# Attention scores of a hybrid decoder trunk: two PSUM banks per unit reduced, exponentiated and summed as one

## The chip, the cores and the metric

The kernel runs on one core of one Trainium2 chip. The metric is the time of one execution on the device in microseconds (us); lower is better. Five engines work from queues of their own, each in order: TensorE (PE, with its weight loads shown apart as PEld), VectorE (DVE), ScalarE (ACT), GpSimd (POOL) and SyncE (SP, which issues DMAs). Matmul results go to PSUM, which the kernel hands out as eight banks of 512 float32 columns by 128 partitions.

## The reference

Two layers over a sequence of 1024 tokens and a width of 1024. Each layer projects the normalised input once, runs three mixers side by side (a gated MLP over chunks, a state space mixer over chunks, and latent attention), joins them with an output projection, and adds a squared-ReLU MLP. All of it is float32. The change is in attention: six heads, query and key width 96, value width 64, blocks of 128 queries:

```python
def one_block(args):
    q_blk, blk = args
    s = jnp.einsum('bhqd,bkhd->bhqk', q_blk, k).astype(jnp.float32) * scale
    q_pos = blk * CHUNK + jnp.arange(CHUNK)
    s = jnp.where(k_pos[None, :] <= q_pos[:, None], s, -jnp.inf)
    p = jax.nn.softmax(s, axis=-1).astype(v.dtype)
    return jnp.einsum('bhqk,bkhd->bqhd', p, v)

out = lax.map(one_block, (qb, jnp.arange(nq)))
```

## The kernel before

Every float32 product is made of three matmuls on operands that are split into a high and a low part (`split`: ScalarE rounds the high part, VectorE subtracts). Most of the time goes to the output projection and the MLP (L1014); attention lies between the projections of a layer and its MLP.

Attention works on units (h,qt): head h of 6, query tile qt of 8, with w = 128 (qt + 1) keys each. A unit with qt of 0 to 3 is narrow and fits one PSUM bank of 512 columns. A unit with qt of 4 to 7 is wide and takes two banks, each with half of its keys. `scores` does a unit: three matmuls per bank, named `sc`, and one more that adds the causal mask to the last 128 keys; a VectorE maximum per bank (L767); for a wide unit a VectorE minimum of the two negated maxima (`mx`); a ScalarE exponential per bank that also sums its row (L780, with a reading of the accumulator of its own). `normalize` adds the two sums (`sm`), takes the reciprocal and multiplies the row, on POOL for all but qt 0. Then `p_t` transposes pieces of up to 512 columns of the result on TensorE (`pTp`) and splits them (`pT`), and `p_v` multiplies them by the values (`av`); a finished half of a head is copied out by ScalarE (`mixC`).

Units are issued in a fixed sequence: (0,0) to (0,3), and then for each head h (h,4), (h,5), (h+1,0), (h,6), (h,7), (h+1,1), (h+1,2), (h+1,3). Beside the first four, `q_tile` projects the last four of eight query tiles (`qps`, evacuated by ScalarE) and `prep_q0` transposes the first head's queries (`qT0`, which the profile shows as `qT`); later heads' queries are transposed eight tiles at a time (`qTp`), and near the end of attention `mix_a` transposes results of the other mixers (`mT`). Normalisation follows four units behind the scores (LAG), and p_v three pieces behind p_t (VKEEP).

The eight PSUM banks are handed out by tag: four to `a`, two to `b`, two to `c`. A bank is written again only when the readers of its last use are done. In attention the tag `a` serves `sc`, `qps`, `qTp` and `mT`; `b` serves `pTp` and `qT0`; `c` serves `av`. Outside of attention all eight banks serve the projections and the MLP.

The order in which each engine's instructions stand is not the order of the source: a scheduler plays the recorded program through with its own costs, takes what is ready first, and fixes one order for each engine. On the chip every engine follows that order and waits by semaphores.

Of the kernel before, what the change touches and what calls it, by code (L numbers as in the profile page):

```python
# [9 lines left out]
F32 = mybir.dt.float32  # L10
# [52 lines left out]
AHEAD = 2  # L63
MIX_FROM = 36


@with_exitstack
def trunk(ctx, tc, x, w_zdk, w_uv, w_f, w_q, w_kv, w_out, w1, w2, gains, pcol, prow, w_s, cst, out):
# [6 lines left out]
    gp = ctx.enter_context(tc.tile_pool(name="gp", bufs=N_G))  # L75
    ps = ctx.enter_context(tc.tile_pool(name="ps", bufs=2, space=PSUM))
    dram = ctx.enter_context(tc.tile_pool(name="dram", bufs=1, space=DRAM))

# [8 lines left out]
    def bank(tag, name):  # L87
        return ps.tile([P, 512], F32, tag=tag, name=name, bufs=BANKS[tag])

# [537 lines left out]
    def qkv(L):  # L627
# [27 lines left out]
        attention_setup(L)  # L655
        L.wq = weights(2, 0)

    def v_tile(L, t, o):
# [15 lines left out]
    def q_tile(L, t):  # L674
        cT, qv = L.cT, L.att[0]
        for n in range(2):
            o = bank("a", "qps")
            for k in range(3):
                whi, wlo = (q_[:, k * 288:(k + 1) * 288] for q_ in L.wq[n])
                a, b = (q_[:, t * P:(t + 1) * P] for q_ in cT[k])  # L680
                on = o[:, 0:288]
                mm(on, a, whi, k == 0, False)
                mm(on, a, wlo, False, False)
                mm(on, b, whi, False, k == 2)
            act.activation(qv[:, t, n * 288:(n + 1) * 288], o[:, 0:288], AF.Copy, scale=L.cr_q[:, t:t + 1])
# [40 lines left out]
    def prep_q(L, h):  # L726
# [3 lines left out]
        for half in range(2):  # L730
            pt = bank("a", "qTp")
            for t in range(4):
                tk = half * 4 + t
                pe.transpose(pt[0:r, t * P:(t + 1) * P], qv[:, tk, (h + 1) * QK - r:(h + 1) * QK], ident)
            sl = slice(half * 512, half * 512 + 512)
            split(qT[i][0][0:r, sl], qT[i][1][0:r, sl], pt[0:r])
# [7 lines left out]
    def attention(L, l, xsrc):  # L744
        vt = L.vt

        def scores(h, qt):
# [7 lines left out]
            wh = w // nh  # L755
            os = [bank("a", "sc") for _ in range(nh)]
            q0 = slice(qt * P, (qt + 1) * P)
            mx = small.tile([P, 2], F32, tag="mx", name="mx", bufs=8)
            for n in range(nh):
                on = os[n][:, :wh]  # L760
                ks = slice(n * wh, (n + 1) * wh)
                mm(on, qh[:, q0], kh[:, ks], True, False)
                mm(on, qh[:, q0], kl[:, ks], False, False)
                mm(on, ql[:, q0], kh[:, ks], False, n < nh - 1)
                if n == nh - 1:
                    mm(on[:, wh - P:], ident_r, maskq_r, False, True)
                dve.reduce_max(mx[:, n:n + 1], on, axis=AX.X, negate=True)  # L767
            if nh == 2:
                tt(mx[:, 0:1], mx[:, 0:1], mx[:, 1:2], ALU.min)
            sm = small.tile([P, 2], F32, tag="sm", name="sm", bufs=8)  # L770
            p0 = 0
# [6 lines left out]
            pw = p[:, p0:p0 + w]  # L778
            for n in range(nh):
                act.activation(pw[:, n * wh:(n + 1) * wh], os[n][:, :wh], AF.Exp, bias=mx[:, 0:1],  # L780
                               accum_out=sm[:, n:n + 1])
            return pw, sm, nh

        narrow = [None]

        def normalize(u, pw, sm, nh):
            if nh == 2:
                tt(sm[:, 0:1], sm[:, 0:1], sm[:, 1:2], ALU.add)
            sm = sm[:, 0:1]
            dve.reciprocal(sm, sm)  # L790
# [94 lines left out]
        for _ in mixing:  # L885
            pass
        R = mlp(L, l, xsrc)
        R.prep(1)
# [8 lines left out]
    def mix_a(L):  # L897
# [3 lines left out]
        for k in range(5):  # L901
            mk = G(F32, "mixA")
            for half in range(2):
                pt = bank("a", "mT")
                for t in range(4):
# [348 lines left out]
    for l in range(DEPTH):  # L1254
# [46 lines left out]
        del L.vv, L.wsv, L.vg, L.sg, L.dtb, L.alog, L.dsk  # L1301
        L = attention(L, l, xsrc).go()


# [73 lines left out]
```

## Time and profile before

| What | us |
|---|---|
| Time, median of 2 runs (2200.74 to 2202.67) | 2201.7 |
| The profiled execution's own time | 2201.31 |
| Its span, first to last instruction | 2199.5 |
| TensorE (PE) busy | 2171.2 |
| Weight loads (PEld) busy | 1846.9 |
| VectorE (DVE) busy | 1661.8 |
| ScalarE (ACT) busy | 1138.0 |
| POOL busy | 477.2 |

The profile is of one execution, which took 1.8 us more than its span. Times on a timeline count from the start of the span. Matmuls are pipelined: a row lasts from the start of one matmul to its last result, and the next one starts before that, so that a busy TensorE is not one at its peak, and its rows hide short waits.

### The profile page before, as it was taken

Reading aid. Unit: us, or ns where it says so; the run is one execution under the profiler, and the core shown is the slowest. Engines: PE = TensorE matmul, PEld = TensorE weight load, DVE = VectorE, ACT = ScalarE, POOL = GpSimd, SP = SyncE. Lnnn points to the kernel's source line nnn. Section 1 sums busy time; section 2 is a strip of 40 time slices with the busy share of each in tenths; the row PEclk is TensorE's granted clock in tenths of the full one; section 3 lists DMA queues with packets and bytes.
Section 4 is the critical chain, followed back from the end, with each engine's and each line's share of the span. In section 5 each row is a group of like instructions: output and inputs, shape, how many; then the busy total and the mean of one; then the engine's idle time right before and its main releaser. Section 6 shows DMA issues by size and latency. Waiting matters only on the chain.

```text
span 2199.5 us, 28731 instructions
## 1 busy us (share of the span) xinstructions
PE 2171.2 (99%) x10844; PEld 1846.9 (84%) x10844; DVE 1661.8 (76%) x2484; ACT 1138.0 (52%) x1867; POOL 477.2 (22%) x451
## 2 busy tenths in 40 slices
PE   9999999999999999999999999999999999999997
PEld 8888989888888888888898889998888888888886
DVE  7788588888776876767847867878888767677576
ACT  6364477556445445355533625775464453553543
POOL 4152266221010001001301613761110010011002
PEclk9999999999999999999999999999999999999999
DMA  5211301445565546545412113023565565356532
GB/s 175 75 53 57 87 1 48 98 125 138 121 130 138 128 100 140 147 89 125 156 50 70 54 45 75 1 96 68 135 153 122 106 140 147 88 125 144 136 75 77
DMA packets 64922, 222.16 MB, mean 101 GB/s; under 512 B 7600, under 2 KB 7952, under 8 KB 64784
## 3 DMA queue, kind: packets, MB, share of 16 engines
q0 software_dynamic: 20736, 75.51, 20.2%
q1 hardware_dynamic: 44048, 144.83, 19.9%
q8 instruction: 85, 1.39, 0.3%
q14 instruction: 53, 0.43, 0.1%
HBM read 211.87 MB, written 8.44 MB: 100 GB/s over the span
## 4 chain that ended last, share of the span: by engine, by line
PE 93%; DVE 4%; issue 2%; ACT 1%; DMA 1%; POOL 0%; SPq 0%; POOLq 0%; ACTq 0%; DVEq 0%
PE st L1014 60%; PE cqkv L119 5%; PE xbc L119 5%; PE uvps L119 4%; PE av L119 4%; PE sc L119 3%; PE zps L119 2%; PE pTp L805 2%; PE qps L119 2%; PE yps L119 1%; PE vps L119 1%; PE knps L119 1%; DVE hB L103 1%; DMA x<-in_x 1%; DVE mx L767 1%
## 5 line engine op out<-in xcount | busy, mean ns | idle before, releaser
L1014 PE MATMUL st<-bhi,wlo 128*128 128x512 f32 x2016 | 785.1, 389 | 0.0
L1014 PE MATMUL st<-blo,whi 128*128 128x512 f32 x2016 | 785.0, 389 | 0.0
L1014 PE MATMUL st<-bhi,whi 128*128 128x512 f32 x2016 | 778.1, 390 | 2.4 <-ACT bhi L115 2.4
L1014 PEld LDWEIGHTS st<-bhi,whi 128*128 128x128 f32 x2016 | 378.7, 188 | 81.1 <-ACT bhi L115 2.7
L1014 PEld LDWEIGHTS st<-blo,whi 128*128 128x128 f32 x2016 | 378.9, 188 | 78.7 <-DVE blo L100 0.5
L1014 PEld LDWEIGHTS st<-bhi,wlo 128*128 128x128 f32 x2016 | 378.7, 188 | 78.5
L206 POOL DMA_DIRECT2D ssum<-in_w x96 | 84.1, 876 | 937.5 <-DVE wlo L100 387.5
L100 DVE TENSOR_TENSOR wlo<-raw,whi 128x1024 fp32r<-128x1024 f32 (+4 forms) x189 | 237.2, 1256 | 54.2 <-issue 29.8
L100 DVE TENSOR_TENSOR x<-x,st 128x512 f32<-128x512 f32 x296 | 196.7, 683 | 30.2 <-PE st L1014 29.8
L115 ACT CAST bhi<-tsum 128x1024 fp32r<-128x1024 f32 x96 | 101.0, 1052 | 213.9 <-DVE tsum L100 172.9
L115 ACT CAST whi<-raw 128x1024 fp32r<-128x1024 f32 (+4 forms) x189 | 193.9, 1029 | 16.0 <-DVE blo L100 12.3
L107 POOL TENSOR_SCALAR p<-p,sm 128x1024 f32<-128x1024 f32 (+6 forms) x84 | 158.9, 1901 | 113.0 <-DVE sm L790 81.3
L115 ACT CAST whi<-ssum 128x1024 fp32r<-128x1024 f32 x108 | 113.4, 1050 | 116.3 <-DMA ssum<-in_w 50.2
L100 DVE TENSOR_TENSOR wlo<-ssum,whi 128x1024 fp32r<-128x1024 f32 x108 | 132.1, 1223 | 49.9 <-ACT whi L115 28.9
L100 DVE TENSOR_TENSOR blo<-tsum,bhi 128x1024 fp32r<-128x1024 f32 x96 | 117.4, 1223 | 46.7 <-ACT bhi L115 46.3
L119 PE MATMUL av<-pT,vhi 128*128 128x256 f32 x480 | 113.5, 298 | 0.7 <-DVE pT L100 0.4
L1059 ACT ACTIVATE hid<-hid 128x1024 f32<-128x1024 f32 x64 | 67.8, 1060 | 87.0 <-DVE hid L1052 86.8
L1052 DVE CUSTOM_DVE_ANT_0 hid<-st,hid 128x512 f32<-128x512 f32 x96 | 65.3, 689 | 56.3 <-PE st L1014 55.9
L119 PE MATMUL sc<-B 96*128 96x384 f32 (+11 forms) x432 | 100.9, 351 | 3.2 <-ACT p L780 1.9
L100 POOL TENSOR_TENSOR sq<-sq 128x512 f32<-128x512 f32 x44 | 67.0, 1528 | 159.7 <-ACT sq L1071 157.6
L780 ACT ACTIVATE p<-sc,mx 128x512 f32<-128x512 f32 (+3 forms) x144 | 83.3, 583 | 20.7 <-DVE mx L100 14.2
L100 DVE TENSOR_TENSOR blo<-hB,bhi 128x1024 fp32r<-128x1024 f32 x48 | 58.7, 1223 | 46.5 <-ACT bhi L115 46.5
(248 smaller groups left out, 3649.7 us busy)
## 6 DMA issues: line engine op xcount, KB each, us to landing
raw<-in_w SPq DMA_DIRECT2D x128, 512.0 KB, 3.9
ssum<-in_w POOLq DMA_DIRECT2D x96, 512.0 KB, 5.7
ssum<-in_w SPq DMA_DIRECT2D x32, 512.0 KB, 4.5
raw<-in_w POOLq DMA_DIRECT2D x32, 512.0 KB, 7.9
raw<-in_w_f SPq DMA_DIRECT2D x20, 512.0 KB, 3.8
raw<-in_w_out SPq DMA_DIRECT2D x16, 512.0 KB, 3.6
dec<-adr SPq DMA_DIRECT2D x16, 384.0 KB, 3.4
ssum<-in_w_out POOLq DMA_DIRECT2D x12, 512.0 KB, 5.8
```

Source lines behind the costliest of these rows:

```text
L100: (eng or dve).tensor_tensor(out=o, in0=a, in1=b, op=op)
L103: dve.scalar_tensor_tensor(out=o, in0=a, scalar=s, in1=b, op0=op0, op1=op1)
L107: (eng or dve).tensor_scalar(out=o, in0=a, scalar1=s1, scalar2=None, op0=op0)
L115: act.copy(hi, src)
L119: pe.matmul(o, lhsT=l, rhs=r, start=start, stop=stop)
L206: pool.dma_start(out=o, in_=src, accum_op=ALU.add)
L767: dve.reduce_max(mx[:, n:n + 1], on, axis=AX.X, negate=True)
L780: act.activation(pw[:, n * wh:(n + 1) * wh], os[n][:, :wh], AF.Exp, bias=mx[:, 0:1], accum_out=sm[:, n:n + 1])
L805: pe.transpose(pt[:, c0:c0 + P], pp[j][:, kt * P:(kt + 1) * P], ident)
L1014: pe.matmul(os[j], lhsT=w[:, cw], rhs=b[:, cb], start=first and n == 0, stop=last and n == 2, skip_group_check=True)
L1052: dve._custom_dve(TENSOR_ADD_SAT, out=d, in0=os[j], in1=d, s0=0.0 if full[0] else BIGGEST, s1=-BIGGEST if full[0] else 0.0)
L1059: act.activation(d, d, AF.Square)
```

## The change

During attention the four banks of tag `a` become two pairs of adjacent banks (`a_banks`, `bank_pair`). A wide unit takes one pair: its seven matmuls fill both banks, and then one VectorE maximum, one ScalarE exponential and one row sum run over both; the minimum and the addition go away. The narrow units (h,0) and (h,1) share one pair, one bank each, and so do (h,2) and (h,3); `spair` holds the pair from the first of the two to the second. `qps`, `qTp` and `mT` move to the two banks of tag `b`, where `pTp` and `qT0` are. The pairs exist from the end of `qkv` to the end of attention; outside of it `a` has four single banks as before.

```diff
+QB, MB = "b", "b"
...
+    psa = []
+
+    def a_banks(pairs):
+        if psa:
+            psa.pop()[0].__exit__(None, None, None)
+        if pairs is not None:
+            cm = tc.tile_pool(name="psa", bufs=2 if pairs else 4, space=PSUM)
+            psa.append((cm, cm.__enter__(), pairs))
+
+    a_banks(False)
...
     def bank(tag, name):
-        return ps.tile([P, 512], F32, tag=tag, name=name, bufs=BANKS[tag])
+        if tag != "a":
+            return ps.tile([P, 512], F32, tag=tag, name=name, bufs=BANKS[tag])
+        if psa[0][2]:
+            return bank_pair(name)[:, 0:512]
+        return psa[0][1].tile([P, 512], F32, tag="a", name=name)
+
+    def bank_pair(name):
+        return psa[0][1].tile([P, 1024], F32, tag="aa", name=name)
...
+        a_banks(True)
...
     def q_tile(L, t):
-            o = bank("a", "qps")
+            o = bank(QB, "qps")
...
-            pt = bank("a", "qTp")
+            pt = bank("b", "qTp")
...
             w = (qt + 1) * P
             nh = 1 if w <= 512 else 2
             wh = w // nh
-            os = [bank("a", "sc") for _ in range(nh)]
+            if nh == 2:
+                o = bank_pair("sc").rearrange("p (n w) -> p n w", n=2)[:, :, 0:wh]
+                os = [o[:, n] for n in range(2)]
+            else:
+                if qt % 2 == 0:
+                    spair[h] = bank_pair("sc")
+                o = (spair[h] if qt % 2 == 0 else spair.pop(h))[:, qt % 2 * 512:qt % 2 * 512 + w]
+                os = [o]
             q0 = slice(qt * P, (qt + 1) * P)
-            mx = small.tile([P, 2], F32, tag="mx", name="mx", bufs=8)
-            for n in range(nh):
-                on = os[n][:, :wh]
+            mx = small.tile([P, 1], F32, tag="mx", name="mx", bufs=8)
+            for n, on in enumerate(os):
                 ks = slice(n * wh, (n + 1) * wh)
                 mm(on, qh[:, q0], kh[:, ks], True, False)
                 mm(on, qh[:, q0], kl[:, ks], False, False)
                 mm(on, ql[:, q0], kh[:, ks], False, n < nh - 1)
-                if n == nh - 1:
-                    mm(on[:, wh - P:], ident_r, maskq_r, False, True)
-                dve.reduce_max(mx[:, n:n + 1], on, axis=AX.X, negate=True)
-            if nh == 2:
-                tt(mx[:, 0:1], mx[:, 0:1], mx[:, 1:2], ALU.min)
-            sm = small.tile([P, 2], F32, tag="sm", name="sm", bufs=8)
+            mm(os[-1][:, wh - P:], ident_r, maskq_r, False, True)
+            dve.reduce_max(mx, o, axis=AX.XY if nh == 2 else AX.X, negate=True)
+            sm = small.tile([P, 1], F32, tag="sm", name="sm", bufs=8)
             p0 = 0
             if qt in (1, 3):
                 p, p0 = narrow[0], qt * P
...
                 if qt < 4:
                     narrow[0] = p
             pw = p[:, p0:p0 + w]
-            for n in range(nh):
-                act.activation(pw[:, n * wh:(n + 1) * wh], os[n][:, :wh], AF.Exp, bias=mx[:, 0:1],
-                               accum_out=sm[:, n:n + 1])
-            return pw, sm, nh
+            pn = pw.rearrange("p (n w) -> p n w", n=2) if nh == 2 else pw
+            act.activation(pn, o, AF.Exp, bias=mx, accum_out=sm)
+            return pw, sm
+        spair = {}
...
-        def normalize(u, pw, sm, nh):
-            if nh == 2:
-                tt(sm[:, 0:1], sm[:, 0:1], sm[:, 1:2], ALU.add)
-            sm = sm[:, 0:1]
+        def normalize(u, pw, sm):
             dve.reciprocal(sm, sm)
             ts(pw, pw, sm, ALU.mult, eng=pool if u[1] > 0 else dve)
             return pw
...
+        a_banks(False)
...
-                pt = bank("a", "mT")
+                pt = bank(MB, "mT")
```

Since the scheduler orders the new program anew, instructions of attention stand in another order on every engine. In the rows below, a number after a name is that of the tile, `sc_2956` one tile of scores for instance, and the last figure is the shape of the output.

On TensorE, the scores of unit (1,7) and what follows, before. `sc_2986` is the second bank of (1,7), `sc_3018` unit (2,1):

```order
L119 MATMUL sc_2986<-B2_2265 128x512 x3
L119 MATMUL sc_2986<-maskq_r_79,ident_r_78 128x128
L805 MATMUL pTp_2970<-cs_77,p_2726 128x128
L805 MATMUL pTp_2970<-cs_77,p_2749 128x128 x2
L119 MATMUL av_2876<-pT_2924,vhi_2117 128x256
L119 MATMUL av_2876<-pT_2924,vlo_2118 128x256
L119 MATMUL av_2876<-pT_2924,vhi_2117 128x256 x2
L119 MATMUL av_2876<-pT_2924,vlo_2118 128x256
L119 MATMUL av_2876<-pT_2944,vhi_2117 128x256
L119 MATMUL sc_3018<-B2_2265 128x256 x3
L119 MATMUL sc_3018<-maskq_r_79,ident_r_78 128x128
L805 MATMUL pTp_3002<-cs_77,p_2690 128x128 x3
```

The same place after: `sc_2956` is the pair of (1,7), `sc_3008` the pair of (2,2) and (2,3), which gets the same banks as `sc_2956`:

```order
L137 MATMUL sc_2956<-B2_2268 128x512 x6
L137 MATMUL sc_2956<-maskq_r_82,ident_r_81 128x128
L137 MATMUL av_2856<-pT_2942,vhi_2120 128x256
L824 MATMUL pTp_2992<-cs_80,p_2790 128x128 x4
L137 MATMUL av_2856<-pT_2942,vhi_2120 128x256
L137 MATMUL av_2856<-pT_2942,vlo_2121 128x256
L137 MATMUL av_2856<-pT_2942,vhi_2120 128x128 x2
L137 MATMUL av_2856<-pT_2942,vlo_2121 128x128
L137 MATMUL sc_3008<-B2_2268 128x384 x3
L137 MATMUL sc_3008<-maskq_r_82,ident_r_81 128x128
```

Both halves of (1,7) now stand together, and (2,1) has moved ahead of them. Between the last scores of (1,7) and the first of (2,2) are six av matmuls of two widths and four transposes.

On ScalarE, around the exponentials of unit (1,7) (`p` is the row of exponentials, `B` the keys and queries), before:

```order
L115 CAST B2_2265<-B1_2086 64x1024
L808 CAST pT_2971<-pTp_2970 128x384
L780 ACTIVATE p_2999,sm_2998<-sc_2985,mx_2987 128x512
L780 ACTIVATE p_2999,sm_2998<-sc_2986,mx_2987 128x512
L808 CAST pT_3003<-pTp_3002 128x384
L780 ACTIVATE p_2941,sm_3025<-sc_3018,mx_3019 128x256
L115 CAST B2_2265<-qTp_3113 128x512
```

The same place on ScalarE after:

```order
L827 CAST pT_2942<-pTp_2941 128x384
L133 CAST B2_2268<-B1_2089 64x1024
L852 COPY mixC_2778<-av_2856 64x512
L802 ACTIVATE p_2967,sm_2966<-sc_2956,mx_2957 128x1024
L827 CAST pT_2970<-pTp_2969 128x384
L827 CAST pT_2993<-pTp_2992 128x512
L802 ACTIVATE p_2916,sm_2990<-sc_2908,mx_2984 128x256
```

One exponential of 1024 columns stands for two of 512. The copy `mixC` of the finished half of a head has come to stand ahead of it; it reads `av_2856`, which the av matmuls of the fence above finish.

On TensorE at the first units, where the query projections stand, before. A name in brackets is the semaphore that the instruction waits for:

```order
L119 MATMUL sc_2513<-B2_2265 128x256
L119 MATMUL sc_2513<-B2_2265 128x256 [waits DVE_49]
L119 MATMUL sc_2513<-maskq_r_79,ident_r_78 128x128
L741 MATMUL qT0_2551<-cs_77,B1_2086 96x128
L741 MATMUL qT0_2607<-cs_77,B1_2086 96x128
L119 MATMUL qps_2522<-whi_2087,chi_1848 128x288 [waits Activation_49]
L119 MATMUL qps_2522<-wlo_2088,chi_1848 128x288
```

And after:

```order
L137 MATMUL qps_2485<-wlo_2292,chi_2030 128x288
L137 MATMUL qps_2485<-whi_2291,clo_2031 128x288
L760 MATMUL qT0_2503<-cs_80,B1_2089 96x128 [waits Activation_49]
L137 MATMUL qps_2528<-whi_2090,chi_1851 128x288 [waits Activation_49]
L137 MATMUL qps_2528<-wlo_2091,chi_1851 128x288
L137 MATMUL qps_2528<-whi_2090,clo_1852 128x288
```

Before, the first head's query tiles were transposed two at a time ahead of a projection. After, one transpose (`qT0_2503`) stands between the last matmul of a projection (`qps_2485`) and the first of the next one (`qps_2528`), and that one gets the bank of `qps_2485` and waits for ScalarE to evacuate it.

## Rows read from the trace of the kernel before

**Rows 1.** The page: busy time of each engine, and the chain that ended last.
```profile
PE 2171.2 (99%) x10844; PEld 1846.9 (84%) x10844; DVE 1661.8 (76%) x2484; ACT 1138.0 (52%) x1867; POOL 477.2 (22%) x451
...
PE 93%; DVE 4%; issue 2%; ACT 1%; DMA 1%; POOL 0%; SPq 0%; POOLq 0%; ACTq 0%; DVEq 0%
```

**Rows 2.** Stretches: us, busy PE, PEld, DVE, ACT, POOL (rows), clock, DMA share, GB/s.
```profile
270.00:300.00 30.00, 27.51 (x190) 24.94 (x189) 24.27 (x82) 20.64 (x61) 15.43 (x9) 1.00 0.00 1
300.00:385.00 85.00, 85.00 (x666) 82.79 (x665) 70.31 (x183) 66.72 (x174) 56.05 (x31) 1.00 0.09 32
```

**Rows 3.** What the weight loader waited for, 270 to 300 us: total, times, longest.
```profile
PEld sc L119 <- ACT p L780: 2.0, 4, 0.9
PEld qTp L734 <- ACT p L780: 1.1, 2, 0.6
PEld sc L119 <- DVE B L100: 0.8, 1, 0.8
PEld av L119 <- DVE pT L100: 0.5, 1, 0.5
```

**Rows 4.** Timeline at 292 us, scores of unit (1,3) behind (0,7): start, length, engine.
```profile
291.21 0.68 ACT L780 ACTIVATE p<-sc,mx 128x512 f32<-128x512 f32 x1
...
291.79 0.19 ACT L780 ACTIVATION_READ_ACCUMULATOR p<-sc,mx 128x1 f32 x1
...
292.03 0.53 PEld L119 LDWEIGHTS sc<-B 128*128 128x128 f32 x3 [0.90 <-ACT p L780]
```

**Rows 5.** VectorE by shape, 255 to 395 us: count | busy us, mean ns | idle before.
```profile
L767 DVE TENSOR_REDUCE mx<-sc 128x1 f32<-128x512 f32 x18 | 12.3, 682 | 0.0
L100 DVE TENSOR_TENSOR pT<-pTp,pT 128x384 fp32r<-128x384 f32 x21 | 11.5, 548 | 0.6 <-ACT pT L808 0.5
...
L767 DVE TENSOR_REDUCE mx<-sc 128x1 f32<-128x320 f32 x12 | 5.8, 482 | 1.3 <-PE sc L119 1.2
...
L100 DVE TENSOR_TENSOR mx<-mx 128x1 f32<-128x1 f32 x24 | 4.3, 181 | 0.1
...
L100 DVE TENSOR_TENSOR sm<-sm 128x1 f32<-128x1 f32 x24 | 3.8, 157 | 4.7 <-ACT p L780 4.7
```

**Rows 6.** ScalarE by shape, 255 to 395 us, as above.
```profile
L780 ACT ACTIVATE p<-sc,mx 128x512 f32<-128x512 f32 x18 | 12.3, 686 | 3.9 <-DVE mx L100 1.6 <-DVE mx L767 1.5 <-DVE sm L790 0.7
...
L808 ACT CAST pT<-pTp 128x384 fp32r<-128x384 f32 x21 | 10.1, 479 | 0.1
...
L780 ACT ACTIVATE p<-sc,mx 128x320 f32<-128x320 f32 x12 | 6.2, 528 | 1.8 <-DVE mx L100 1.4 <-DVE sm L790 0.3
...
L833 ACT COPY mixC<-av 64x512 f32<-64x512 f32 x10 | 5.8, 582 | 2.6 <-PE av L119 2.5
```

**Rows 7.** Timeline of TensorE at 307 us: end of the scores of unit (1,7).
```profile
306.34 0.40 PE L119 MATMUL av<-pT,vhi 128*128 128x256 f32 x2
...
306.82 0.85 PE L119 MATMUL sc<-B 128*128 128x512 f32 x3
...
307.51 0.22 PE L119 MATMUL sc<-maskq_r,ident_r 128*128 128x128 f32 x1
...
307.56 0.50 PE L805 MATMUL pTp<-cs,p 128*128 128x128 f32 x3
```

**Rows 8.** Timeline at 278 us: a reduction, its exponential, an evacuation of a projection.
```profile
277.94 0.56 DVE L767 TENSOR_REDUCE mx<-sc 128x1 f32<-128x384 f32 x1
...
278.54 0.58 ACT L780 ACTIVATE p<-sc,mx 128x384 f32<-128x384 f32 x1 [0.19 <-DVE mx L767]
...
279.25 0.50 ACT L685 ACTIVATE B<-qps,ry 128x288 f32<-128x288 f32 x1
```

**Rows 9.** Timeline of ScalarE at 310 us: second exponential of unit (1,7).
```profile
310.47 0.68 ACT L780 ACTIVATE p<-sc,mx 128x512 f32<-128x512 f32 x1
```

**Rows 10.** Stretches early in the MLP of layer 1, columns as in rows 2.
```profile
1577.00:1581.00 4.00, 2.29 (x16) 2.01 (x15) 3.56 (x8) 2.23 (x5) 0.00 (x0) 1.00 1.04 230
1581.00:1590.00 9.00, 9.00 (x38) 7.39 (x38) 7.47 (x10) 1.53 (x2) 0.54 (x1) 0.81 0.28 97
```

More of the change, by code (lines that the diff above doesn't have):

```diff
@@ L1302, in trunk @@
         L = attention(L, l, xsrc).go()
+    a_banks(None)
 def kernel(**inputs):
```

## Prediction

> **What bounds the kernel now.** I read the busy shares and the chain first: the reader is to see TensorE busy 99% of the span and 93% of the chain that ended last, the other engines a few per cent [rows 1]. So a change to VectorE and ScalarE work pays only where TensorE waits for them. The table of stretches shows where that is [rows 2]. Attention of layer 0 runs from 255 to 395 us; layer 1 runs the same code. TensorE is busy 27.51 of 30 us from 270 to 300 (the start of the scores) and 85.00 of 85 from 300 to 385. In that full stretch VectorE is busy 70.31 us (83%) and ScalarE 66.72 (78%): loaded, not full. A matmul's row outlasts its step (the mask row lasts 0.22 us, the next matmul starts after 0.05 [rows 7]), so short waits hide; the weight loader's waits show them whole: 2.0 + 1.1 + 0.8 + 0.5 = 4.4 us a layer from 270 to 300 [rows 3], with no entry at all from 300 to 385. Most of it waits for an exponential that frees a score bank. The largest single one shows the pattern: an exponential and its reading of the accumulator end at 291.98, the weight load that needed the bank starts at 292.03 [rows 4].
>
> **What the change takes away.** Call (h,qt) the unit of head h and query tile qt; qt 4 to 7 is wide (two banks). From the rows by shape, a reduction takes 0.48 us at 320 columns and 0.68 at 512: 1.04 ns a column and 0.15 fixed [rows 5]. An exponential takes 0.53 at 320 and 0.69 at 512: 0.82 ns a column and 0.27 [rows 6]. A wide unit loses one fixed part on each, the minimum (0.18), the addition (0.16) and a reading of the accumulator (0.19, mostly beside the end of the exponential [rows 4]). VectorE gains 0.15 + 0.18 + 0.16 = 0.49 us, and 24 wide units a layer make 11.8 us; ScalarE gains about 0.25 x 24 = 6 us. Where TensorE is full this is worth nothing. Where it waits, it is worth at most the 4.4 us a layer above.
>
> **What it adds.** The order after is fixed, so between the last matmul of a unit and the first that needs its banks again I count the TensorE steps that stand there, the cover, and set against it the time until the banks are free, the need. Steps, from TensorE's own rows: 0.23 us for 512 columns, 0.12 for a 256-column av, 0.11 for a transpose, 0.05 to 0.06 for 128 columns [rows 7]. The need is: 0.16 for the matmul's tail, the reduction, the exponential, 0.14 from the end of the exponential to the next weight load (291.89 to 292.03), and two handoffs of 0.04; the handoff is that from the reduction's end to the exponential (277.94 + 0.56 to 278.54) [rows 4, 8]. That is 0.38 + R + E. No reduction or exponential over two banks is in the trace; I extend the two lines above (1024: 1.21 and 1.11; 896: 1.08 and 1.00; 768: 0.95 and 0.90). Needs: 2.70 us at 1024, 2.46 at 896, 2.23 at 768, 1.75 at 512.
>
> *A, the pair after qt 7.* Only two pairs exist, and the narrow units (h+1,0) and (h+1,1) hold one of them while (h,6) and (h,7) go through the other. So (h+1,2) takes the pair that (h,7) has just filled. In the order, (1,2) stands straight behind (0,7): cover 0, wait 2.70. For the next three heads the cover is three av steps of 256, four transposes and three steps of 128: 0.36 + 0.44 + 0.18 = 0.98. There a copy of av (0.58 [rows 6]) stands before the exponential on ScalarE and itself waits for the last of those av steps: 0.98 + 0.16 + 0.04 + 0.58 + 0.04 = 1.80 until the exponential starts, later than the reduction would allow (1.45), so the need is 1.80 + 1.11 + 0.14 = 3.05 and the wait 2.07. For head 5 the cover is 1.31 and the wait 1.39. Sum a layer: 2.70 + 3 x 2.07 + 1.39 = 10.3 us; without the copy 9.3. Before, the two banks of (h,7) were two of four, and the same count gives covers of 5.1 and 3.8 us there. A rule of the Trainium skill speaks against the merge in the same sense (Perfetto Trace Analysis, Optimizing Scalar/DVE Operations): where Scalar and Vector are not saturated but cause bubbles elsewhere, splitting instructions may finish work sooner. The change does the reverse; the rule gives no price.
>
> *B, other units with a short cover.* (0,5) behind (0,3): cover 1.59, need 1.75. (0,6) behind (0,5): three transposes, four narrow score steps and two transposes, 0.70, need 2.23. (0,7) behind (0,6): 1.73, need 2.46. (1,5) behind (1,3): 1.27, and (5,5) behind (5,3): 1.48, both need 1.75. Sum 0.16 + 1.53 + 0.73 + 0.48 + 0.27 = 3.2 us.
>
> *C, projections on two banks.* qps moves from four banks to the two of tag b, beside the transposes of q. In units (0,0) to (0,3) one transpose (0.11) is all that stands between a projection and the next one, or the next transpose, that needs its bank. The evacuation on ScalarE takes 0.50 [rows 8], with the tail and two handoffs of 0.05: 0.16 + 0.05 + 0.50 + 0.05 = 0.76. Four waits of 0.65: 2.6 us.
>
> *D, the last 384-column piece of a head.* The transposes of q to tag b push the last pTp of a head behind them, and its av follows too closely: cover 0.68 us to the second av matmul, which needs the cast (0.48) and the subtraction (0.55) [rows 5, 6]: 0.16 + 0.48 + 0.55 + 3 x 0.04 = 1.31. Wait 0.63, four heads: 2.5 us.
>
> What hides nothing else: the waiting scores stand at the head of TensorE's queue, and av, the transposes and the next scores wait behind them; POOL's normalisation and the weight DMAs have four units of lead.
>
> **The sum.** Per layer 10.3 + 3.2 + 2.6 + 2.5 = 18.6 us added, 4.4 taken away (every wait of the start is among B's or gone): net 14.2, for two layers 28.4. The profiled execution takes 2201.31 us (span 2199.5), 0.4 under the median of two, 2201.7: 2201.3 + 28.4 = 2229.7, so **2230 us**. Bounds. Low: no copy in the way (9.3), C at 2.0 if evacuations start early, D free, B without its smallest two: 9.3 + 2.7 + 2.0 - 4.4 = 9.6, twice 19: 2220. High: a queue before VectorE and ScalarE. Before, in the full stretch, (1,7) shows it: its last matmul starts at 307.51 and its second exponential ends at 311.15, 3.64 us, where 0.22 + 0.68 + 0.18 + 2 x 0.69 + 0.12 = 2.58 would do [rows 7, 9]. One more us on each of the ten waits in A and B: 24.2 a layer, 2250. I take the value near the low end of that, since an engine that TensorE has let run out has no queue.
>
> **Rivals.** *Relief wins (faster).* The lighter VectorE and ScalarE bring every maximum forward, and the start's waits vanish: 2201.3 - 2 x 4.4 = 2192.5. It holds if the covers suffice, that is if both banks together need no more than 0.98 us after the last matmul instead of 2.70; the fixed parts are only 0.42 of the 2.32 us of R + E, which says no. Halfway, with the cost of a column half of what the lines say on two banks (need 0.38 + 0.68 + 0.69 = 1.75), A is 1.75 + 3 x 0.77 + 0.44 = 4.5 and B 1.5: 6.7 net with C and D, 2215. The Trainium skill (the same section) says that grouping can improve throughput if the engine is saturated; at 83% VectorE is not.
> *Waits breed waits (slower by over 2%).* Every stall of TensorE delays pTp, and the in-order queues of ScalarE (casts among exponentials) and POOL stretch needs that I counted bare; also the granted clock may fall. It does so early in the MLP of layer 1: from 1577 to 1581 TensorE was busy 2.29 of 4 us, and in the next 9 us the mean grant was 0.81, so part of them at 1.2 instead of 2.4 GHz [rows 10]; that costs 0.19 x 9 = 1.7 us. Twice the waits of A and B and a fall at each of A's: 32.1 + 8.5 - 4.4 = 36 a layer, 2274. It decides from 0.8 us more on each of the ten places of A and B: 8 us a layer more than the forecast pass 2245.7.
> *The pairs don't bind:* if the release were by half, as before, A would shrink to its second half and the time stay near 2210.
>
> **How the numbers follow.** Forecast (2216 to 2245) 0.65, waits that breed 0.17, half cost or half release (2202 to 2216) 0.13, relief 0.05. The range, **2212 to 2254**, reaches into both neighbours and leaves out about 2 in 10. Two per cent, about what a measurement of this kernel tells from no change, is 44 us. Faster by that: 0.01, there are not 44 us of waits to win. Slower: over 2245.7, 0.17 and a little of the forecast's upper edge: 0.19. Within: 0.80.
>
> **What would show it.** After: TensorE no longer 85 of 85 us in the middle of attention but with one wait of about 2 us a head, 18 us apart, named as waiting for the exponential, just before the scores of (h+1,2); reductions of 1.2 and exponentials of 1.1 us; VectorE lighter by some 12 us a layer; four waits of 0.6 before qps or the transposes of q; the stage after attention unchanged. Wrong if the two-bank reduction is much faster than the line, if the waits of the start go without new ones, or if the clock's row falls under 1 in attention.

## The result and the profile after

The changed kernel takes 2258.8 us (median of two, 2256.4 to 2261.2) against 2201.7 before: a ratio of 1.026, 95% interval 1.0245 to 1.0279, slower by 57 us. The forecast was 2230 with a range up to 2254. The direction and the main new wait were right, the size was half.

The page of the kernel after, first the busy times, then the chain; the last line is the group of score matmuls, with the idle time just before them:

```profile
PE 2196.9 (97%) x10844; PEld 1864.2 (83%) x10844; DVE 1652.8 (73%) x2340; ACT 1129.5 (50%) x1771; POOL 475.5 (21%) x451
...
PE 90%; DVE 4%; ACT 3%; issue 2%; DMA 0%; POOL 0%; SPq 0%; POOLq 0%; ACTq 0%; DVEq 0%
...
L137 PE MATMUL sc<-B 96*128 96x384 f32 (+11 forms) x432 | 103.8, 366 | 23.1 <-ACT p L802 22.9
```

VectorE and ScalarE do less, as forecast: 144 and 96 instructions fewer. By the rows of the groups, VectorE's maxima, minima and additions fell from 79.0 + 8.6 + 7.5 us to 70.5, and ScalarE's exponentials with their readings of the accumulator from 83.3 + 29.0 to 71.5 + 19.1. The busy times of the page, where rows that overlap count once, fell by 9.0 and 8.5 only. TensorE, with the same 10844 matmuls, has gaps. The stretches of attention in layer 0 show where, with the columns of [rows 2]:

```profile
270.00:300.00 30.00, 24.29 (x147) 21.21 (x147) 18.82 (x60) 15.51 (x41) 11.95 (x7) 0.94 0.00 1
300.00:385.00 85.00, 76.44 (x546) 71.95 (x544) 55.48 (x110) 51.45 (x113) 48.36 (x27) 0.96 0.00 1
```

Against [rows 2], TensorE's 85.00 of 85 us are now 76.44 (546 matmuls stand in the stretch where 666 stood), VectorE's 70.31 are 55.48, and the mean granted clock, 1.00 before in both, is 0.94 and 0.96. The weight loader's waits from 255 to 430 us name the cause (total, times, longest):

```profile
PEld sc L137 <- ACT p L802: 13.9, 13, 2.8
PEld qps L137 <- ACT B L704: 3.1, 4, 0.8
PEld st L1034 <- ACT bhi L133: 2.3, 1, 2.3
PEld pTp L824 <- issue: 1.8, 4, 0.6
PEld av L137 <- DVE pT L118: 1.4, 4, 0.4
```

All rows of that view together make 26.8 us, against 7.3 in the same stretch before: 19.5 us more a layer, where the forecast had 14.2 net. The five places of term A are in the timeline of the weight loader, in brackets what each first load of (h+1,2) waited:

```profile
298.04 0.47 PEld L137 LDWEIGHTS sc<-B 128*128 128x128 f32 x3 [2.82 <-ACT p L802]
...
321.01 0.47 PEld L137 LDWEIGHTS sc<-B 96*128 96x128 f32 x3 [2.04 <-ACT p L802]
...
343.67 0.47 PEld L137 LDWEIGHTS sc<-B 128*128 128x128 f32 x3 [2.04 <-ACT p L802]
...
367.15 0.47 PEld L137 LDWEIGHTS sc<-B 96*128 96x128 f32 x3 [2.04 <-ACT p L802]
...
392.83 0.47 PEld L137 LDWEIGHTS sc<-B 128*128 128x128 f32 x3 [1.34 <-ACT p L802]
```

They sum to 10.3 us, the 10.3 of the forecast. The timeline at the third of them shows the chain that it counted: mask matmul, maximum (the 1.55 is a narrow one and this one in a row), the copy of av, the exponential straight behind it, the load 0.15 us after its end:

```profile
340.41 0.22 PE L137 MATMUL sc<-maskq_r,ident_r 128*128 128x128 f32 x1
...
340.68 1.55 DVE L791 TENSOR_REDUCE mx<-sc 128x1 f32<-128x1024 f32 x2 [1.59 <-PE sc L137]
...
341.80 0.58 ACT L852 COPY mixC<-av 64x512 f32<-64x512 f32 x1
...
342.41 1.11 ACT L802 ACTIVATE p<-sc,mx 128x1024 f32<-128x1024 f32 x1
```

By shape, a reduction of 1024 columns takes 1.22 us and an exponential 1.11; the lines drawn from one bank gave 1.21 and 1.11:

```profile
L791 DVE TENSOR_REDUCE mx<-sc 128x1 f32<-128x1024 f32 x6 | 7.3, 1222 | 7.7 <-PE sc L137 7.7
...
L802 ACT ACTIVATE p<-sc,mx 128x1024 f32<-128x1024 f32 x6 | 6.7, 1114 | 2.6 <-DVE mx L791 2.5
```

What the forecast's sum had no entry for is the clock. Two stretches around that wait and one around the same unit of layer 1:

```profile
340.00:344.00 4.00, 2.10 (x16) 1.87 (x15) 2.84 (x4) 3.22 (x6) 1.04 (x2) 1.00 0.00 0
344.00:348.00 4.00, 4.00 (x20) 3.87 (x19) 2.50 (x6) 1.98 (x6) 4.00 (x3) 0.59 0.00 0
...
1457.00:1461.00 4.00, 3.75 (x16) 3.76 (x17) 2.66 (x7) 2.55 (x9) 3.45 (x2) 0.57 0.00 0
```

TensorE is busy 2.10 of 4 us, and in the next 4 it is full at a mean grant of 0.59: most of that time at 1.2 instead of 2.4 GHz. Over the whole span, apart from its last microseconds, the record of the granted clock has 30.7 us at the lower level in nine places, against 3.4 us in one place before (that of [rows 10]). Half of the extra 27.3 us, 13.7, is my estimate of what they cost.

### The profile page after: what moved, and what is told of

Same layout as the page of the kernel before. It is cut to its first block, busy times and chain, and to the rows that moved or that the text cites. A ratio compares the mean times of both kernels' runs of the same rounds, so it can differ in the third digit from the quotient of the medians.

```text
span 2254.6 us, 28409 instructions
## 1 busy us (share of the span) xinstructions
PE 2196.9 (97%) x10844; PEld 1864.2 (83%) x10844; DVE 1652.8 (73%) x2340; ACT 1129.5 (50%) x1771; POOL 475.5 (21%) x451
## 3 DMA queue, kind: packets, MB, share of 16 engines
q0 software_dynamic: 20736, 75.51, 19.5%
q8 instruction: 85, 1.39, 0.2%
## 4 chain that ended last, share of the span: by engine, by line
PE 90%; DVE 4%; ACT 3%; issue 2%; DMA 0%; POOL 0%; SPq 0%; POOLq 0%; ACTq 0%; DVEq 0%
PE st L1034 59%; PE cqkv L137 5%; PE xbc L137 5%; PE uvps L137 4%; PE sc L137 4%; PE av L137 3%; PE zps L137 2%; PE pTp L824 2%; PE qps L137 2%; ACT p L802 1%; PE yps L137 1%; PE knps L137 1%; PE vps L137 1%; DVE hB L121 1%; DVE mx L791 1%
## 5 line engine op out<-in xcount | busy, mean ns | idle before, releaser
L125 POOL TENSOR_SCALAR p<-p,sm 128x256 f32<-128x256 f32 (+6 forms) x84 | 158.0, 1887 | 161.2 <-DVE sm L809 137.3
L137 PE MATMUL av<-pT,vhi 128*128 128x256 f32 x480 | 121.4, 312 | 1.9 <-DVE pT L118 1.2
L118 DVE TENSOR_TENSOR pT<-pTp,pT 128x512 fp32r<-128x512 f32 (+1 forms) x120 | 75.4, 635 | 39.9 <-ACT pT L827 39.2
L137 PEld LDWEIGHTS sc<-B 96*128 96x128 f32 (+1 forms) x432 | 74.4, 200 | 32.6 <-ACT p L802 28.3
```

The source lines that it names most:

```text
L118: (eng or dve).tensor_tensor(out=o, in0=a, in1=b, op=op)
L125: (eng or dve).tensor_scalar(out=o, in0=a, scalar1=s1, scalar2=None, op0=op0)
L137: pe.matmul(o, lhsT=l, rhs=r, start=start, stop=stop)
```

## The experiments

Two theories stood at the start. W: TensorE's new waits for banks make the time, first those for a pair that is held too long (term A). M: the merged instructions themselves do, wherever the banks are. A third question was the clock (K), a fourth the bank moves of `qps`, `qTp` and `mT`. "Over before" is the ratio to runs of the kernel before on the same chip, times 2201.7. Each edit also lets the scheduler order every engine's instructions anew, so that no run changes one thing alone.

**e1: the kernel before with the bank moves alone** (four single score banks, nothing merged).

```diff
-            o = bank("a", "qps")
+            o = bank("b", "qps")
...
-            pt = bank("a", "qTp")
+            pt = bank("b", "qTp")
...
-                pt = bank("a", "mT")
+                pt = bank("b", "mT")
```

> The kernel before, with its four single score banks and its two maxima and two exponentials, and with only the projections qps, the query transposes qTp and the transposes mT moved to the two banks of tag b. Theory W (the new waits of TensorE for banks cost the time, at the places where the covers are short): the five waits of the projections (3 x 0.75 + 0.76 + 0.69 = 3.7 us a layer in the trace of the changed kernel) and some of the waits of the transposes (2 to 3 us a layer) appear here too, and no fall of the clock inside the attention: 2202 + 2 x 6 = 2214 us (2208 to 2220). Rival M (the merged instructions over two banks themselves, longer by their latency, cost the time, wherever the banks are): 2202 us, within 4.

2235.8 us, 1.016 (1.0145 to 1.0176). Neither had it: the moves alone cost 35 us. The loader's waits in attention:

```profile
PEld sc L119 <- ACT p L780: 5.1, 9, 1.2
PEld qps L119 <- ACT B L685: 3.1, 4, 0.8
PEld av L119 <- ACT pT L808: 2.6, 5, 1.9
```

The 3.1 at the projections are those of the changed kernel; but the scores' waits for exponentials grew too, from 2.0 [rows 3] to 5.1, av waits 2.6 for its cast, and the time at the lower clock from 3.4 to 13.7 us.

**e2: the changed kernel's pairs and moves, without the merge.**

```diff
-            dve.reduce_max(mx, o, axis=AX.XY if nh == 2 else AX.X, negate=True)
...
+                dve.reduce_max(mx[:, n:n + 1], on, axis=AX.X, negate=True)
+            if nh == 2:
+                tt(mx[:, 0:1], mx[:, 0:1], mx[:, 1:2], ALU.min)
...
-            act.activation(pn, o, AF.Exp, bias=mx, accum_out=sm)
+            for n in range(nh):
+                act.activation(pw[:, n * wh:(n + 1) * wh], os[n], AF.Exp, bias=mx[:, 0:1],
+                               accum_out=sm[:, n:n + 1])
```

> The changed kernel's pairs and bank moves, with two maxima, a minimum, two exponentials and an addition per wide unit as before. Theory W: a pair still comes free only after both halves, some 0.38 + 0.68 + 0.2 + 2 x 0.69 = 2.6 us after the last matmul at 1024 columns, so the unit (h+1, 2) waits as long as with the merge (4 x about 2.5 = 10 us a layer), the clock falls as often, and the relief is gone: 2265 us (2248 to 2285). Rival M: with the merged instructions gone, the time goes back to that of the bank moves alone: 2205 to 2220 us.

2284.0 us, 1.038 (1.0362 to 1.0393), at the upper end of W's range. M falls: at the same banks the merge is worth 25 us. W's places are there, and worse:

```profile
PEld sc L137 <- ACT p L805: 24.0, 18, 2.9
PEld sc L137 <- DVE mx L792: 2.5, 3, 1.2
```

**e4: the pair of the narrow units held for less time**, the merge and the moves as in the change.

```diff
-INTER = ((0, 4), (0, 5), (1, 0), (0, 6), (0, 7), (1, 1), (1, 2), (1, 3))
+INTER = ((0, 4), (0, 5), (0, 6), (0, 7), (1, 0), (1, 1), (1, 2), (1, 3))
```

> The changed kernel with units (h+1, 0) placed behind (h, 7) and no longer ahead of (h, 6), so that the pair of (h+1, 0) and (h+1, 1) is not held while (h, 6) and (h, 7) run; the cover of (h+1, 2) then counts 2.44 us of TensorE's steps and no longer 0.98. Theory W: of the 10.8 us a layer at the pairs some 1.2 are left, the eight falls of the clock (1.7 us each) go with them: 2258.8 - 2 x 9.6 - 13.6 = 2226 us, and up to 5 less if the late starts of the next units were their echo (2214 to 2232). Rival M: the same merged instructions, the same time, 2250 us or more.

2228.4 us, 1.0125 (1.0109 to 1.0140): 30 us off, inside W's range. The loader waits 3.8 us for exponentials where the change has 13.9, and the clock does not fall at all before the end of the span:

```profile
PEld sc L137 <- ACT p L802: 3.8, 9, 0.9
PEld qps L137 <- ACT B L704: 3.1, 4, 0.8
PEld pTp L824 <- DVE pT L118: 3.0, 5, 0.7
```

**e6: that order in the kernel before**, a control (the same edit of `INTER`).

> The kernel before, single banks and all, with the order of units in which (h+1, 0) stands behind (h, 7): the order that took 30 us off the changed kernel. Theory W (that order helped there because a pair was held for a shorter time): nothing comes of it where no pair is held, 2202 us (2197 to 2208). Rival O (the order is the better one in any kernel): 2190 us or less.

2206.2 us, 1.0025 (1.0015 to 1.0035), inside W's range. The order by itself costs 6 us; what it gained in e4 it gained through the pair.

**e8: the change's own order, but no sharing of pairs.**

```diff
-                if qt % 2 == 0:
-                    spair[h] = bank_pair("sc")
-                o = (spair[h] if qt % 2 == 0 else spair.pop(h))[:, qt % 2 * 512:qt % 2 * 512 + w]
+                o = bank_pair("sc")[:, 0:w]
```

> The changed kernel in its own order of units, with a pair of its own for each narrow unit (the second bank of that pair stays unused): no unit shares a pair with its neighbour. The cover of the first units of a head then counts 1.7 us against a need of 1.5 to 1.75, but for head 1, where two covers are 0.7. Theory W: of the 10.8 us a layer some 2 are left, and at most two falls of the clock: 2258.8 - 2 x 8.8 - 6 x 1.7 = 2231 us, and up to 7 less with the echoes (2216 to 2236). Rival M: 2250 us or more. If this one gains and the one with the other order does not, the place of the unit counts and not how long a pair is held.

2228.1 us, 1.012 (1.0105 to 1.0139), inside W's range and the same 30 us by another way. What e4 and e8 share is that no pair is held while (h,6) and (h,7) run: this is the cause of A, not the place of the units.

**e5: useless products in the wait.**

```diff
+            if qt == 2 and h > 0:
...
+                avs[key] = bank("c", "av")
+                for _ in range(FILL):
+                    mm(avs[key][:, 0:384], x[:, 0:P], x[:, 0:384], True, True)
```

> The changed kernel, with ten more products of 384 columns each (10 x 0.176 = 1.76 us at the interval of the trace) right behind the last score product of (h, 7) for three of the four heads that follow one, into the bank that the next values' sums will overwrite from their start: the result is the same, and TensorE computes through the 2.16 us for which (h+1, 2) waits. Theory K (the clock falls because TensorE stands still there): the falls behind these three waits in each layer go, at 1.7 us each, six or seven of eight, and the waits themselves give back 2.16 - 1.76 = 0.4 each: 2258.8 - 10.2 to 11.9 - 2.4 = 2245 us (2241 to 2250). Rival (the falls are not the work of these waits, or they cost nothing): 2254 to 2262 us with the falls where they were.

2250.7 us, 1.022 (1.0207 to 1.0238): 49 over before, 8 less than the change, 0.7 above K's range and 3.3 under the rival's. The expectation counted the filling wrong: it stands at five units a layer, not three. In four it lies in the wait (2.04 three times and 1.34); at (1,2) it came behind it. So 10 x 1.76 = 17.6 us of products were added and 2 x (3 x 2.04 + 1.34) = 14.9 of waits went, and yet the time fell by 8.1: 10.8 us came from elsewhere. The time at the lower clock fell from 30.7 to 10.2 us, and half of that fall is 10.2. All five falls behind waits that were filled are gone; the one at (1,2) of layer 1, where the filling came behind the wait, stayed. Of the others, two at the MLP went, and one came at 300 us, where the filling of (1,2) stands behind its wait. In the code, `key` is the next av tile and `x` the transposed piece that av takes next. In the timeline of layer 0, the filling follows the last score product of (2,7):

```profile
342.70 0.22 PE L138 MATMUL sc<-maskq_r,ident_r 128*128 128x128 f32 x1
...
342.77 1.95 PE L138 MATMUL av<-pT 128*128 128x384 f32 x10
```

In the stretch behind it the grant stays 1.00, where the change had 0.59:

```profile
344.00:348.00 4.00, 4.00 (x32) 4.00 (x31) 3.42 (x8) 3.65 (x9) 2.19 (x1) 1.00 0.00 0
```

**e10, e11, e12: one bank move each** in the kernel before, as the three lines of e1's diff.

> The kernel before, with the query projections qps alone on the two banks of tag b. All three bank moves together gave 2235.8 us, 35 over the kernel before. Theory Q (the projections' waits, and what they put late in head 0): most of the 35 is here, 2202 + 2 x (3.7 at the projections themselves + 4 to 8 behind them in head 0) = 2217 to 2226 us. Rival R (the transposes qTp and mT, which share the two banks with the transposes pTp of every head): only the 3.7 us a layer of the projections themselves, 2209 us, within 4.

> The kernel before, with the query transposes qTp alone on the two banks of tag b. Theory Q (the projections cost most of the 35 us): 2202 to 2208 us. Rival R (the transposes do): 2210 to 2220 us, with waits of pTp or of the scores for B behind qTp once a head.

> The kernel before, with the transposes mT of the mixing alone on the two banks of tag b; they run in the last third of the attention. Theory Q: 2202 to 2208 us. Rival R: 2208 to 2218 us, with the late starts behind 365 us of the span.

`qps` alone gave 2215.9 us (1.0065, 1.0049 to 1.0082), `qTp` alone 2222.9 (1.0094, 1.0079 to 1.0109), `mT` alone 2211.5 (1.0042, 1.0027 to 1.0057): 14, 21 and 9 us, 44 together against 35 in one kernel. Theory Q (the projections) falls. R holds in that all three cost and the transposes most, though `qTp` and `qps` each came out some us above what R gave. In e10, 3.9 us of new waits a layer are at the projections and the transpose beside them, as in the change, and 2.7 more at the scores behind them, waiting for their exponential. In e11 the moved transposes hardly wait; the growth is at the scores. First e10, then e11:

```profile
PEld sc L119 <- ACT p L780: 4.7, 4, 2.5
PEld qps L119 <- ACT B L685: 3.1, 4, 0.8
```

```profile
PEld sc L119 <- ACT p L780: 7.0, 9, 2.2
```

In e12 a part is clock: at the end of attention TensorE waits 2.3 us for the MLP's first operand (1.3 before), and the clock falls, as the two stretches show:

```profile
393.00:396.00 3.00, 1.25 (x5) 0.86 (x5) 1.79 (x3) 3.00 (x7) 0.86 (x1) 1.00 0.00 0
396.00:400.00 4.00, 3.98 (x11) 3.08 (x11) 2.84 (x5) 2.07 (x4) 0.00 (x0) 0.57 0.48 139
```

**e9, e7, e13, e14: the moved tiles on tag `c`.** e9 is e4, and e7 is e8, with `qps` on `c`; e13 is e4 with all three there, as in the diff; e14 is e4 with the two transposes there.

```diff
-QB, MB = "b", "b"
+QB, MB = "c", "c"
...
-            pt = bank("b", "qTp")
+            pt = bank("c", "qTp")
```

> The changed kernel with that order of units (2228.4 us), and the projections qps on the two banks of tag c, which hold the values' sums, in place of tag b. Theory W: the 3.7 us a layer at the projections go, and what they put late in head 0 with them: 2213 to 2221 us. Rival (the wait moves to the value projections vps, which are on tag c): 2225 us or more.

> The changed kernel in its own order, with a pair of its own for every narrow unit (2228.1 us), and qps on tag c. Theory W: the projections' 3.7 us a layer go and one or two falls of the clock: 2214 to 2221 us. Rival (the wait moves to vps): 2225 us or more.

> The changed kernel with that order of units, and qps, qTp and mT all on tag c, so that tag b holds pTp alone, and qT0, as before the change. Theory S (of the 27 us left in that version, the sharing of tag b with pTp costs the most): 2198 to 2212 us. Rival (tag c is held by the values' sums until a copy has emptied it, so the same waits come there): 2222 us or more.

> The changed kernel with (h+1, 0) behind (h, 7) (2228.4 us), qps on tag b, and the transposes qTp and mT on tag c. Theory S (the transposes, which share tag b with pTp, cost the most; alone they gave 21 and 10 us): 2206 to 2215 us. Rival (tag c is as bad a place, since the values' sums hold it): 2222 us or more.

e9: 2237.7 us (1.0168), e7: 2233.0 (1.0147); both worse than with `qps` on `b`, on the rival's side by their times. But the waits are not at the value projections that the rival named: one projection waits 1.8 us, and 24 us are at the lower clock. e13: 2220.8 (1.0091) and e14: 2220.2 (1.0088), 8 us better than e4 and between the two theories' ranges: taking the transposes away from `pTp` gives back 8 of the 27 us, not all.

**e17, e16: the projections in the pairs.** e17 is e4, with the two projections of a query tile in one pair; e16 has the transposes on `c` as well.

```diff
+        qp = bank_pair("qps")
         for n in range(2):
-            o = bank(QB, "qps")
+            o = qp[:, n * 512:n * 512 + 512]
```

> The changed kernel with (h+1, 0) behind (h, 7), qTp and mT on tag b, and each query tile's two projections in the two banks of one pair. Theory Q (the projections' 3.7 us a layer and what they put late in head 0): 2214 to 2221 us. Rival (the tiles take the pairs from the first units of head 0, and the same waits come there): 2226 us or more.

> The changed kernel with (h+1, 0) behind (h, 7), the projections in the pairs, and the transposes qTp and mT on tag c: tag b holds what it held before the change. If the 27 us are the bank moves alone, 2196 to 2207 us, at or under the kernel before. If the pairs keep a part of their own (units whose cover is under 1.7 us), 2210 us or more.

2233.6 (1.0149) and 2225.6 us (1.0112). e17 is worse than e4 and e16 worse than e14, both on the side of the higher range. They don't answer the question: the first projection now waits 3.6 us a layer. The profile names no releaser; as I read the code, the pairs can take the place of the single banks only when all four are free.

**e18, e19: four banks in turn, no pool of pairs**, given out in the order of the code through the whole kernel, merged and not. Outside of attention more of these tiles are in use at once than the turn allows, so, as I read the code, later products overwrite sums that are still to be read: that part of the computation is changed.

```diff
...
+    def bank_pair(name):
+        k = (spot[0] + 1) // 2 * 2 % 4
+        spot[0] = (k + 2) % 4
+        return four[:, k * 512:(k + 2) * 512]
...
```

> The merged instructions, with no pool of pairs and no bank moves: the four banks of tag a as one tile, given out in turn, a wide unit two neighbours, all else one bank. Theory W (only the waits for banks made the change slow; the merge itself relieves the start of the scores): the relief of at most 4.4 us a layer against a few short covers, 2194 to 2206 us, and 5 to 25 us under the version with two of each instruction. Rival T (banks given out in the order of the code stand in each other's way, merged or not): 2212 us or more, both alike.

> The same turns of the four banks, with two maxima, a minimum, two exponentials and an addition per wide unit as before the change. Theory W: 2203 to 2222 us, over the merged version by 5 to 25 us. Rival T: 2212 us or more, and within 4 us of the merged version.

2612 and 2684 us: far over W, and on T's side, though T had both alike. Banks in a fixed turn cost 18% and 22%; that they do so by keeping TensorE's work in the order of the code is argued, not shown. The pair of runs agrees with e2 that merging at the same banks is a gain, here 72 us where TensorE waits everywhere. A version that beats the kernel before was not found; e14, the best with the merge, is 19 us over it.

Two readings of each trace account for nearly all of these times: the rise of the weight loader's waits in attention of layer 0 (all rows of that view, from 250 to 430 us, in e2 to 445), doubled for two layers (layer 1 of the change has 27.5 for the 26.8), and half of the extra time at the lower clock, which is an estimate. All in us:

```
kernel                     waits  lower clock   2 x rise + half   measured over before
before                       7.3          3.4                 -                      -
after                       26.8         30.7       39.0 + 13.7                   57.7
e1  moves alone             20.2         13.7       25.8 +  5.1                   35.4
e2  pairs, no merge         40.3         58.0       66.0 + 27.3                   83.0
e4  pair held short         20.3          0.0       26.0 -  1.7                   27.5
e6  order alone              9.1          0.0        3.6 -  1.7                    5.5
e8  no sharing              18.1         10.2       21.6 +  3.4                   26.9
e10 qps                     13.3         10.2       12.0 +  3.4                   14.3
e11 qTp                     13.2         17.1       11.8 +  6.8                   20.7
e12 mT                      10.1         13.7        5.6 +  5.1                    9.2
e7  e8, qps on c            18.0         23.9       21.4 + 10.2                   32.4
e9  e4, qps on c            20.6         23.9       26.6 + 10.2                   37.0
e13 e4, all three on c      13.7         20.5       12.8 +  8.5                   20.0
e14 e4, transposes on c     14.1         17.1       13.6 +  6.8                   19.4
e16 e14, qps in pairs       16.2         17.1       17.8 +  6.8                   24.7
e17 e4, qps in pairs        21.4         13.7       28.2 +  5.1                   32.8
```

The two readings come within some 5 us of the measured time, except in e2, where they give 10 too much.

## Why the prediction was right in direction and half in size

*What bounds the kernel* held: by their rows VectorE and ScalarE lost 24.6 and 21.7 us over two layers, and where TensorE was full it was worth nothing. The forecast was 23.6 and some 12; ScalarE's readings of the accumulator make the difference. That *relief* is the one gain was right as well, but its bound of 4.4 us a layer, read from the waits of the kernel before, was too low once the banks are scarce: at the changed kernel's banks the merge gives 25 us (e2). It pays there for a part of what the banks cost. That splitting would let work finish sooner is not borne out at these banks.

*A* was right in place, mechanism and size: 2.82, three of 2.04 and 1.34 against 2.70, 2.07 and 1.39, with the copy of av ahead of the exponential as counted. Removing it in two ways took 30 us off. The loader's waits of both layers fell by 13 us in e4 and 17 in e8, less than A's 20.6, since small waits grew; half of the time at the lower clock fell by 15 and 10.

*B* was 3.2 a layer and is about 1.3, with 0.86 more at a transpose ahead of (0,6). But four waits of 0.24 to 1.02 us came where the covers had looked long enough, 2.3 us. The queue on VectorE and ScalarE that I had put only into the upper bound would explain them; I have not traced each.

*C and D, the bank moves,* are the term of the sum that was mis-sized. I priced 5.1 us a layer, each move by the waits at its own tile, and no wait for `mT`. In the trace after, C is 3.8 (a fifth place at the first projection), and the waits of D's kind are 3.2, of which 1.5 stood before. Alone in the kernel before, though, the moves cost 35 us, 17 a layer (e1): transposes and scores behind them come late, and those wait again for their exponentials. I don't claim which queue passes it on in each place; e10 to e12 show only that each of the three moves does it. With A gone, 27 us are left (e4), where the forecast without A is 2 x (3.2 + 2.6 + 2.5 - 4.4) = 7.8; 8 of the 27 go when the transposes leave tag `b` (e14). How the other 19 divide between the projections, the pairs' short covers and the clock stays open, since e16 and e17, made for it, met a new wait.

*The sum* failed in a second place: it left the clock at full speed and put its fall into a rival, "waits breed waits", with a chance of 0.17. A clock under 1 in attention, which the prediction named as a sign of being wrong, is what came (0.94 and 0.96). There are eight more falls than before, 13.7 us by the estimate above. Six of them come right behind waits of A, two in layer 0 and four in layer 1, at about the 1.7 us each that [rows 10] gave; four of A's ten waits were followed by none. Of the other two, one comes ahead of A's first wait, at 290 us, where e1 has one without any pairs, and one behind the wait for the MLP's first operand in layer 1. That wait is 2.3 us where it was 1.3, so the stage after attention does not start unchanged, as the prediction had it. The rival's other half, twice the waits of A and B, did not come.

So of the 29 us missing, 13.7 are the clock (e5 gave about 10 of it back), 2 x (19.5 - 14.2) = 10.6 are waits beyond the forecast, and some 5 show in neither reading; late starts too short for the loader's waits may be among them. The experiments divide the same 29 in another way: A cost 30 us with the falls behind it where its waits alone were 20.6, 10 more, and the rest cost 27 where the forecast had 7.8, some 20 more.

## What to carry to other kernels

Merging two instructions over two banks gains what it promises on VectorE and ScalarE, but the banks then come free together and later; count for each next user the steps of TensorE that cover the wait, and also who holds the other pair meanwhile. A tile that moves to another set of banks must be priced by a run or by the whole chain behind it, not by the wait at its own instruction. Where waits of about 2 us are forecast on a TensorE that was full before, a fall of its clock behind them belongs into the sum: here it followed six of ten such waits.

## What the runs showed of the hardware

A maximum over two adjacent banks and an exponential over two banks follow the line of one bank: 1.22 and 1.11 us at 1024 columns. Six of A's ten waits, of 2.04 to 2.82 us, were followed by TensorE's lower clock (grant 0.57 to 0.59 in the next 4 us) in a stretch that was otherwise full, and useless products in the wait kept the grant at 1.00. It is no rule for each wait of that length. The longest, 2.82 us ahead of (1,2), was followed by a fall in layer 1 of the changed kernel and by none in layer 0; first layer 0, then layer 1:

```profile
298.00:302.00 4.00, 3.66 (x26) 3.46 (x27) 1.97 (x6) 1.31 (x4) 3.63 (x2) 1.00 0.00 0
...
1409.00:1413.00 4.00, 3.73 (x16) 3.50 (x17) 1.77 (x6) 1.12 (x4) 3.74 (x2) 0.59 0.00 0
```

And in e4, with TensorE busy 1.86 of 4 us ahead of the MLP, the grant stayed at 1.00, where e12's 1.25 of 3 us at the same place was followed by 0.57:

```profile
402.00:406.00 4.00, 1.86 (x12) 1.45 (x10) 1.67 (x2) 3.23 (x6) 1.75 (x1) 1.00 0.01 5
406.00:410.00 4.00, 3.99 (x19) 3.14 (x18) 2.96 (x5) 2.18 (x4) 0.00 (x0) 1.00 0.46 136
```
